# A decoder trunk with stick-breaking attention: scores by pairs of heads with q and k unstacked, and query blocks 0 and 1 as one unit

## The chip, the cores and the metric

The kernel runs on 1 core of one Trainium2 chip. The metric is device time in microseconds (us), from the start of one execution to its end. The kernel before was run three times.

## What is computed

The reference runs two layers over a residual stream of 512 positions by 1024. The first is multi-head latent attention with a causal softmax (called the MLA layer here). The second is stick-breaking attention with 16 heads of 64, which takes its keys and values from a product of the stream after the first layer. After each layer a gated embedding is added: `x + sigmoid(x @ W) * (p @ W')`. The change touches the second layer, whose core is this, for each block of 128 queries of each head:

```python
z = einsum('bhqd,bhkd->bhqk', qi, k) * scale
mask = s_idx[None, :] < t_idx[:, None]
log_beta = log_sigmoid(z)
log_one_minus = where(mask, log_sigmoid(-z), 0.0)
tail = cumsum(log_one_minus, reverse=True) - log_one_minus
a = where(mask, exp(log_beta + tail), 0.0)
o = einsum('bhqk,bhkd->bhqd', a, v)
```

Then `x + (o * silu(gate)) @ w_out`. All is float32.

## The kernel before, in words

Activations lie transposed: features on the 128 partitions, 512 positions along the free axis. A float32 product is made of three matmuls in the reduced format `float32r`, after each operand is split in two parts, high and low: high by high, high by low, low by high (`mm3`, L121 to L123). ScalarE (ACT) makes the high part by a cast, VectorE (DVE) or GpSimd (POOL) the low part by a subtraction (`split_w` for weights, L130 and L131; `split_act` for activations, L147 and L148).

The second layer goes in four groups of four heads. For each group `sb_group` makes values (`V`), keys and queries by products with weights that POOL first multiplies by a gain (L169 and L614). The products of the next group and the gate products (`gate2`) are handed out as filler, a chunk at a time, between the steps of the attention of the current group (`layer`, `windows`); after the last group the embedding product and the two big output products follow (`pp_gemm`, `out_ple`).

*Keys and queries before.* A head has 64 features, half of the 128 rows. The kernel stacks parts along the rows: for a key tile the upper half holds the high part and the lower half the low part (or the other way round), and each query has two tiles, one with the high part in both halves (tag `qk`) and one with the low part in both halves (tag `hat`). Two matmuls of 128 rows then give all products of the parts. Making this takes, for each chunk of two heads, two casts and two subtractions of 64 rows for the keys (L588 to L591) and four casts and four subtractions of 64 rows for the queries (L601 to L604).

*Attention before.* One step is one query block `j` (0 to 3) of one head (`sb_front`): two matmuls of (j+1)*128 columns, at least 256, into one of two PSUM buffers of tag `s` (L643, L644); two sigmoids on ACT (L648, L649); a scan from the right on DVE that multiplies the factors up (L650); a product on POOL (L652); and a masking of the diagonal block on POOL (`affine_select`, L653). The tiles have tag `e`, with six buffers, two for each step. Some steps later PE transposes the blocks (`pt_evac`, L522), ACT casts them out of PSUM (L527), DVE subtracts the low part (L528), and when a head's four blocks are there, `av` multiplies them with the values (L542).

The order of the instructions on each engine is set when the program is built: a scheduler with priorities (`high_priority`, `SB_PRIO`, `SB_FILL`) simulates the program and places every instruction. Each engine then runs its own list in order and waits at semaphores.

Of the kernel before, what the change touches and what calls it, by code (L numbers as in the profile page):

```python
# [43 lines left out]
SB_LEAD = (2, 3, 2)  # L44
# [12 lines left out]
SPREAD = "gst"  # L57
SPREAD_PLE = "gstt"

# [25 lines left out]
class Trunk:  # L85
    def __init__(self, ctx, tc, A):
        self.tc, self.nc, self.A = tc, tc.nc, A
        self.cp = ctx.enter_context(tc.tile_pool(name="cp", bufs=1))
        self.sp = ctx.enter_context(tc.tile_pool(name="sp", bufs=1))
        self.pp = ctx.enter_context(tc.tile_pool(name="pp", bufs=1, space=PSUM))  # L90
        self.dp = ctx.enter_context(tc.tile_pool(name="dp", bufs=1, space=DRAM))
        self.n = 0

    BUFS = {"A": 8, "B": 10, "qk": 8, "hat": 6, "gate": 8, "v": 2, "f": 6, "e": 6, "ws": 3, "wh": 2, "wl": 2, "R": 1,
            "sm": 16, "smg": 3, "g": 2, "s": 2, "t": 3, "o": 1}

    def t(self, shape, dt, tag):
        self.n += 1
        return self.sp.tile(shape, dt, tag=tag, name=f"{tag}{self.n}", bufs=self.BUFS[tag])

    def ps(self, shape, tag):
        self.n += 1
        return self.pp.tile(shape, F32, tag=tag, name=f"{tag}{self.n}", bufs=self.BUFS[tag])

    @contextmanager
# [88 lines left out]
    def setup(self):  # L194
# [6 lines left out]
        for _ in range(WARM):  # L201
# [10 lines left out]
                                compare_op=ALU.is_ge, fill=NEG, base=0, channel_multiplier=1)  # L212
        nc.gpsimd.affine_select(out=self.maskb[:, S - P:S], in_=self.maskb[:, S - P:S], pattern=[[-1, P]],
                                compare_op=ALU.is_ge, fill=1.0, base=-1, channel_multiplier=1)
        self.pt = []
        for i in range(2):
            pair = []
# [70 lines left out]
    def mla_in(self):  # L288
# [1 line left out]
        gc = self.const([P, NCOL], F32, "gc")  # L290
        self.gc = gc
        MC = (QL + KL) // P
        tags = "".join(x * self.BUFS[x] for x in "gst")
        acc = [self.ps([P, S], x) for x in tags[:MC]]
        xacts = []
        sqx = self.t([P, S], F32, "f")
# [216 lines left out]
    def pt_evac(self, h, j, e):  # L513
        nc = self.nc
        pt = self.pt[h % 2]
        if j == 0:
            self.e0 = e
            return
        blocks = [(self.e0, 0), (e, 0), (e, 1)] if j == 1 else [(e, c) for c in (1, 0, 2, 3)[:j + 1]]
# [3 lines left out]
        if j == 1:  # L523
            views = [x[:, 0:3 * P].rearrange("p (i q) -> p i q", q=P) for x in pt]
        else:
            views = [x[:, 3 * P:PTC].rearrange("p (i q) -> p i q", q=2 * P)[:, 0:j + 1, (j - 2) * P:(j - 1) * P] for x in pt]
# [51 lines left out]
    def sb_group(self, g, res):  # L578
        nc, A, v = self.nc, self.A, self.nc.vector
        ks, qs = {}, {}  # L580

        def k_evac(m, ps):
            kr = self.t([P, S], F32, "f")
            v.tensor_tensor(out=kr, in0=ps, in1=self.R2, op=ALU.mult)
            a = self.t([P, S], F32R, "B")
            b = self.t([P, S], F32R, "B")
            lo, hi = slice(0, HD), slice(HD, P)
            nc.scalar.copy(out=a[lo], in_=kr[lo])  # L588
            nc.scalar.copy(out=b[hi], in_=kr[hi])
            v.tensor_tensor(out=a[hi], in0=kr[lo], in1=f32(a[lo]), op=ALU.subtract)  # L590
            v.tensor_tensor(out=b[lo], in0=kr[hi], in1=f32(b[hi]), op=ALU.subtract)  # L591
            ks[2 * m], ks[2 * m + 1] = a, b

        def q_evac(m, ps):
            qr = self.t([P, S], F32, "f")
            v.tensor_tensor(out=qr, in0=ps, in1=self.R2, op=ALU.mult)
            for i, own in enumerate((slice(0, HD), slice(HD, P))):
                oth = slice(HD, P) if i == 0 else slice(0, HD)
                a = self.t([P, S], F32R, "qk")
                b = self.t([P, S], F32R, "hat")  # L600
                nc.scalar.copy(out=a[own], in_=qr[own])  # L601
                nc.scalar.copy(out=a[oth], in_=qr[own])
                v.tensor_tensor(out=b[own], in0=qr[own], in1=f32(a[own]), op=ALU.subtract)
                v.tensor_tensor(out=b[oth], in0=qr[own], in1=f32(a[own]), op=ALU.subtract)  # L604
                qs[2 * m + i] = (a, b)

        gkv = self.gc[:, C_KVLN:C_KVLN + NK]
        gsb = self.gc[:, C_SBLN:C_SBLN + NK]
# [15 lines left out]
            self.v_evac(V[:, t], ps, self.r2[:, t:t + 1])  # L624
            yield
        for m in (2 * g, 2 * g + 1):
            yield from self.gemm_gen(A["w_k"][m], m, self.x2, k_evac, gkv)
            yield
        for m in (2 * g, 2 * g + 1):
            yield from self.gemm_gen(A["w_sq"][m], m, self.x2, q_evac, gsb)  # L630
            yield
        res[:] = [qs, ks, V]

    def sb_prep(self, h, qs, ks, V):
        return qs[h] + (ks[h], V)

    def sb_front(self, h, j, qa, qb, k, V):
        nc, v = self.nc, self.nc.vector
        n = (j + 1) * P
        nn = max(n, 2 * P)  # L640
        js = slice(j * P, n)
        ps = self.ps([P, S], "s")
        nc.tensor.matmul(ps[:, 0:nn], lhsT=qa[:, js], rhs=k[:, 0:nn], start=True, stop=False)  # L643
        nc.tensor.matmul(ps[:, 0:nn], lhsT=qb[:, js], rhs=k[:, 0:nn], start=False, stop=True)  # L644
        om = self.t([P, S + 8], F32, "e")
        b = self.t([P, S + 8], F32, "e")
        nc.vector.memset(om[:, n:n + 1], 1.0)
        nc.scalar.activation(om[:, 0:n], ps[:, 0:n], AF.Sigmoid, scale=-(HD ** -0.5))  # L648
        nc.scalar.activation(b[:, 0:n], ps[:, 0:n], AF.Sigmoid, scale=HD ** -0.5)  # L649
        v.tensor_tensor_scan(out=om[:, 0:n][:, ::-1], data0=om[:, 0:n][:, ::-1], data1=self.maskb[:, S - n:S][:, ::-1],  # L650
                             initial=1.0, op0=ALU.mult, op1=ALU.max)
        nc.gpsimd.tensor_tensor(out=b[:, 0:n], in0=b[:, 0:n], in1=om[:, 1:n + 1], op=ALU.mult)  # L652
        nc.gpsimd.affine_select(out=b[:, js], in_=b[:, js], pattern=[[-1, P]], compare_op=ALU.is_ge, fill=0.0,  # L653
                                base=-1, channel_multiplier=1)
        return b

    def pp_gemm(self, i):
        nc, A = self.nc, self.A
# [56 lines left out]
    def layer(self, windows, prep, front, pair, prep_lead, lead, av_lag, off):  # L715
# [5 lines left out]
        for i in range(-prep_lead, NS + lead + av_lag):  # L721
            ip = i + prep_lead
            if ip < NS:
                g = ip // GS
                if ip % NT == 0:
                    with hp(offset=off[0]):
                        heads[ip // NT] = prep(ip // NT, *self.groups[g])
                n, gen = windows[g]
                while done[g] * GS < n * (ip % GS + 1):
                    next(gen, None)  # L730
                    done[g] += 1
                if ip % GS == GS - 1:
                    for _ in gen:
                        pass
            if 0 <= i < NS:
                with hp(offset=off[1]):
                    es[i] = front(i // NT, i % NT, *heads[i // NT])
            b = i - lead
            if 0 <= b < NS:
                with hp(offset=off[2]):  # L740
                    self.pt_evac(b // NT, b % NT, es.pop(b))
# [17 lines left out]
    def run(self):  # L759
# [183 lines left out]
```

## Time and profile before

| | us |
|---|---|
| three runs | 710.0, 712.96, 713.29 |
| median | 712.96 |
| span of the profiled execution | 709.4 |
| PE busy | 667.6 |
| DVE busy | 526.7 |
| ACT busy | 409.6 |
| POOL busy | 401.3 |

The span runs from the first to the last instruction of one execution that the hardware profiler took; no time outside the span is recorded for that execution. "Busy" is the time in which at least one instruction ran. A matmul's end is modelled, and consecutive matmuls overlap, so how fast PE gets along is read from the distance between the starts of neighbouring matmuls. PEld are weight loads, each ahead of its matmul. The first scores of the second layer start at 375 us, the last products with the values end at 610 us.

### The profile page before, as it was taken

To read this page: it belongs to the slowest core of one execution; us is meant where nothing else is said; L and a number is where in the kernel's file an instruction comes from. 1 tells how busy PE (TensorE), PEld (TensorE's weight loads), DVE (VectorE), ACT (ScalarE), POOL (GpSimd) and SP (SyncE) were. 2 spreads that over 40 slices of the span, in tenths; PEclk is the share of its full clock that TensorE was granted. 3 is DMA by queue.
4 is the path that set the end of the run, shared out by engine and by line. 5 is a ranking of instruction groups with operands and counts; after the bars stand their busy time and mean duration, and the time that the engine had idled before them with its cause. 6 is when DMAs were issued, how large, how long until landed. Compare 5 with 4: busy or idle time off the path is not lost.

```text
span 709.4 us, 10085 instructions
## 1 busy us (share of the span) xinstructions
PE 667.6 (94%) x3494; PEld 563.9 (79%) x3494; DVE 526.7 (74%) x966; ACT 409.6 (58%) x837; POOL 401.3 (57%) x371
## 2 busy tenths in 40 slices
PE   8899999899999999998898998999999988999997
PEld 6688878788868888887787876878887767888886
DVE  6758499999978866455579899799789788544432
ACT  7266586868878655453254667666466365622321
POOL 6638476775695430058545687787883998200131
PEclk9999999999999999999998999999999999999999
DMA  6232202010133113442231112111112121443231
GB/s 232 78 121 92 93 31 64 30 33 14 32 119 119 46 60 95 135 155 98 84 116 60 60 61 59 61 59 61 61 59 89 61 84 58 147 137 109 84 124 59
DMA packets 21474, 59.28 MB, mean 84 GB/s; under 512 B 2864, under 2 KB 3376, under 8 KB 21424
## 3 DMA queue, kind: packets, MB, share of 16 engines
q1 hardware_dynamic: 21424, 58.65, 25.8%
q8 instruction: 27, 0.44, 0.2%
q14 instruction: 23, 0.19, 0.1%
HBM read 54.45 MB, written 4.19 MB: 83 GB/s over the span
## 4 chain that ended last, share of the span: by engine, by line
PE 42%; DVE 25%; issue 14%; POOL 13%; ACT 4%; DMA 2%; SPq 0%; POOLq 0%; ACTq 0%; DVEq 0%
PE g L121 6%; PE g L123 6%; PE g L122 6%; POOL e L652 4%; PE t L121 3%; PE t L123 3%; PE t L122 3%; PE s L121 3%; PE s L123 3%; PE s L122 3%; POOL e L653 3%; DVE e L650 3%; DVE wl L131 2%; PE o L542 2%; DVE ptl L528 2%
## 5 line engine op out<-in xcount | busy, mean ns | idle before, releaser
L130 ACT CAST wh<-ws 128x1024 fp32r<-128x1024 f32 (+2 forms) x92 | 90.8, 987 | 105.9 <-issue 50.2
L131 DVE TENSOR_TENSOR wl<-ws,wh 128x1024 fp32r<-128x1024 f32 (+2 forms) x72 | 100.9, 1401 | 44.6 <-ACT wh L130 38.3
L121 PE MATMUL g<-A,wh 128*128 128x512 f32 x280 | 112.6, 402 | 4.0 <-ACT wh L322 4.0
L122 PE MATMUL g<-A,wh 128*128 128x512 f32 x280 | 112.4, 401 | 1.0 <-DVE A L148 0.9
L123 PE MATMUL g<-A,wl 128*128 128x512 f32 x280 | 110.7, 399 | 0.4 <-DVE wl L131 0.4
L652 POOL TENSOR_TENSOR e<-e,e 128x128 f32<-128x128 f32 (+1 forms) x64 | 62.4, 983 | 26.9 <-DVE e L650 12.7
L650 DVE TENSOR_TENSOR_SCAN e<-e,maskb 128x128 f32<-128x128 f32 (+1 forms) x64 | 71.1, 1125 | 8.5 <-ACT e L648 6.6
L522 PE MATMUL t<-ident,e 128*128 128x128 f32 x320 | 61.0, 278 | 11.7 <-POOL e L652 6.8
L709 POOL TENSOR_TENSOR f<-f,B 128x512 f32<-128x512 f32 x8 | 14.1, 1765 | 102.2 <-ACT f L707 102.0
L169 POOL TENSOR_TENSOR ws<-ws,gc 128x1024 f32<-128x1024 f32 x24 | 50.3, 2097 | 31.9 <-DMA ws<-in_w_k 10.0
L121 PEld LDWEIGHTS g<-A,wh 128*128 128x128 f32 x280 | 53.3, 190 | 15.0 <-ACT wh L322 5.1
L122 PEld LDWEIGHTS g<-A,wh 128*128 128x128 f32 x280 | 53.5, 191 | 12.1 <-DVE A L148 2.8
L123 PEld LDWEIGHTS g<-A,wl 128*128 128x128 f32 x280 | 53.1, 190 | 10.5 <-DVE wl L131 0.8
L522 PEld LDWEIGHTS t<-ident,e 128*128 128x128 f32 x320 | 39.8, 140 | 24.3 <-POOL e L652 9.6
L528 DVE TENSOR_TENSOR ptl<-t,pth 128x384 fp32r<-128x384 f32 (+1 forms) x96 | 55.1, 589 | 2.5 <-ACT pth L527 2.0
L527 ACT CAST pth<-t 128x384 fp32r<-128x384 f32 (+1 forms) x96 | 47.9, 522 | 7.9 <-PE t L522 7.5
L131 POOL TENSOR_TENSOR wl<-ws,wh 128x1024 fp32r<-128x1024 f32 (+2 forms) x20 | 41.0, 2052 | 18.9 <-ACT wh L130 18.9
L648 ACT ACTIVATE e<-s 128x128 f32<-128x128 f32 (+1 forms) x64 | 28.4, 444 | 35.4 <-POOL e L652 19.7
L568 ACT ACTIVATE e<-e,sm,smg 128x128 f32<-128x128 f32 (+1 forms) x64 | 42.1, 660 | 11.7 <-DVE sm L567 9.3
L653 POOL TENSOR_SCALAR_AFFINE_SELECT e<-e 128x128 f32<-128x128 f32 x64 | 44.8, 711 | 1.5
L572 POOL TENSOR_SCALAR e<-e,sm 128x384 f32<-128x384 f32 (+3 forms) x48 | 28.6, 603 | 26.7 <-DVE sm L570 18.2
L542 PE MATMUL o<-ptl,v 128*128 128x256 f32 (+2 forms) x128 | 40.7, 340 | 1.0 <-DVE ptl L528 1.0
(324 smaller groups left out, 1935.4 us busy)
## 6 DMA issues: line engine op xcount, KB each, us to landing
ws<-in_w_pg SPq DMA_DIRECT2D x16, 512.0 KB, 3.6
ws<-in_w_g SPq DMA_DIRECT2D x8, 512.0 KB, 3.2
ws<-in_w_o SPq DMA_DIRECT2D x16, 256.0 KB, 2.5
ws<-in_w_v SPq DMA_DIRECT2D x8, 512.0 KB, 3.6
ws<-in_w_k SPq DMA_DIRECT2D x8, 512.0 KB, 3.5
ws<-in_w_sq SPq DMA_DIRECT2D x8, 512.0 KB, 3.5
ws<-in_w_sg SPq DMA_DIRECT2D x8, 512.0 KB, 3.6
ws<-in_w_o SPq DMA_DIRECT2D x8, 512.0 KB, 3.6
```

Source lines behind the costliest of these rows:

```text
L121: mm(ps, lhsT=wh, rhs=xh, start=first, stop=False)
L122: mm(ps, lhsT=wh, rhs=xl, start=False, stop=False)
L123: mm(ps, lhsT=wl, rhs=xh, start=False, stop=last)
L130: nc.scalar.copy(out=wh, in_=src)
L131: lo_engine.tensor_tensor(out=wl, in0=src, in1=f32(wh), op=ALU.subtract)
L169: nc.gpsimd.tensor_tensor(out=ws, in0=ws, in1=gain.unsqueeze(2).to_broadcast((P, nk, P)), op=ALU.mult)
L522: nc.tensor.transpose(ps[:, i], src[:, c * P:(c + 1) * P], self.ident)
L528: nc.vector.tensor_tensor(out=views[1], in0=ps, in1=f32(views[0]), op=ALU.subtract)
L542: nc.tensor.matmul(ps[:, q0:S], lhsT=V[:, c, hh], rhs=rhs, start=(c == 0 and i == 0), stop=(c == NT - 1 and i == 1))
L650: v.tensor_tensor_scan(out=om[:, 0:n][:, ::-1], data0=om[:, 0:n][:, ::-1], data1=self.maskb[:, S - n:S][:, ::-1], initial=1.0, op0=ALU.mul ...
L652: nc.gpsimd.tensor_tensor(out=b[:, 0:n], in0=b[:, 0:n], in1=om[:, 1:n + 1], op=ALU.mult)
L653: nc.gpsimd.affine_select(out=b[:, js], in_=b[:, js], pattern=[[-1, P]], compare_op=ALU.is_ge, fill=0.0, base=-1, channel_multiplier=1)
```

## The change

1. Keys and queries are no longer stacked. For a chunk of two heads one tile holds the high parts of both (first head in rows 0 to 63, second in rows 64 to 127) and one the low parts: one cast and one subtraction of 128 rows each (`evac`, `split_act`).
2. Scores are made for two heads at a time (`sb_scores`). For each head there are three matmuls of 64 rows (high by high, high by low, low by high), placed by `tile_position` in rows 0 to 63 for the first head and 64 to 127 for the second, in turn. They write the two halves, one PSUM bank each, of a single tile `s2` that stays for the whole program; the tag `s` elsewhere takes these halves in turn.
3. Query blocks 0 and 1 become one unit of 512 columns (block 0 with key blocks 0 and 1, block 1 with key blocks 0 and 1), with a mask of its own, `maskp`, that makes key block 1 of query block 0 drop out and the scan start anew between the two. A pair of heads thus has three units of 512, 384 and 512 columns for each head, where a head had four steps of 128, 256, 384 and 512. The sigmoids take both heads in one instruction, scans and products stay one for each head, the masking is one for both heads (two for the first unit).
4. The loop is `sb_layer`, with a lead of one unit between scores and transposes; `pt_evac` is called by units in both layers. The `e` tiles hold two heads each, still six of them. The DMA scratch area is set to 1024 (`dynamic_dma_scratch_size`).

```diff
-    def sb_front(self, h, j, qa, qb, k, V):
-        nc.tensor.matmul(ps[:, 0:nn], lhsT=qa[:, js], rhs=k[:, 0:nn], start=True, stop=False)
-        nc.tensor.matmul(ps[:, 0:nn], lhsT=qb[:, js], rhs=k[:, 0:nn], start=False, stop=True)
...
+        def evac(to, tag):
+            def f(m, ps):
+                r = self.t([P, S], F32, "f")
+                v.tensor_tensor(out=r, in0=ps, in1=self.R2, op=ALU.mult)
+                to[m] = self.split_act(r, tag)
...
+    def sb_scores(self, u, qs, ks):
+        ps = self.s2
+        parts = [(0, 0, 2), (1, 2, 2)] if u == 0 else [(u + 1, 0, u + 2)]
+        terms = [(qs[0], ks[0]), (qs[0], ks[1]), (qs[1], ks[0])]
+        for j, c0, nb in parts:
+            for i, (q, k) in enumerate(terms):
+                for hh in range(2):
+                    rows = slice(hh * HD, (hh + 1) * HD)
+                    nc.tensor.matmul(ps[:, hh, c0 * P:(c0 + nb) * P], lhsT=q[rows, j * P:(j + 1) * P],
+                                     rhs=k[rows, 0:nb * P], start=i == 0, stop=i == 2, tile_position=(hh * HD, 0))
+    def sb_front(self, u, ps):
+        n = (4, 3, 4)[u] * P
+        om = self.t([P, 2, S + 8], F32, "e")
+        b = self.t([P, 2, S + 8], F32, "e")
+        v.memset(om[:, :, n:n + 1], 1.0)
+        nc.scalar.activation(om[:, :, 0:n], ps[:, :, 0:n], AF.Sigmoid, scale=-(HD ** -0.5))
+        nc.scalar.activation(b[:, :, 0:n], ps[:, :, 0:n], AF.Sigmoid, scale=HD ** -0.5)
+        for hh in range(2):
+            v.tensor_tensor_scan(out=x, data0=x, data1=mask[:, ::-1], initial=1.0, op0=ALU.mult, op1=ALU.max)
+            nc.gpsimd.tensor_tensor(out=b[:, hh, 0:n], in0=b[:, hh, 0:n], in1=om[:, hh, 1:n + 1], op=ALU.mult)
+        for d in ds:
+            nc.gpsimd.affine_select(out=d, in_=d, pattern=[[0, 2], [-1, P]], compare_op=ALU.is_ge, fill=0.0, base=-1,
+                                    channel_multiplier=1)
...
-        self.layer(windows, self.sb_prep, self.sb_front, pair2, *SB_LEAD, SB_PRIO)
+        self.sb_layer(windows, pair2, SB_LEAD, SB_PRIO)
```

The scheduler places the whole program anew, the first layer too. On PE, at the scores of query block 3 of a head in the second group, the order before has two matmuls of 128 rows (`s`) between products of the filler (`g`):

```order
L121 MATMUL g_5312<-wh_5218,A_3574 128x256
L122 MATMUL g_5312<-wl_5219,A_3574 128x256
L643 MATMUL s_5630<-B_4831,qk_5001 128x512
L644 MATMUL s_5630<-B_4831,hat_5002 128x512
L123 MATMUL g_5312<-wh_5218,A_3574 128x256
```

Now, at the same block of a pair of heads, six matmuls of 64 rows stand in one run between full-row matmuls of the filler (`g`) and of the product with the values (`o`):

```order
L140 MATMUL g_4674<-A_3636,wh_4670 128x512
L141 MATMUL g_4674<-A_3636,wl_4671 128x512
L653 MATMUL s_66<-B_4267,qk_4424 128x512 x2
L653 MATMUL s_66<-B_4268,qk_4424 128x512 x2
L653 MATMUL s_66<-B_4267,qk_4425 128x512 x2
L139 MATMUL g_4674<-A_3677,wh_4670 128x512
L569 MATMUL o_4824<-pth_112,v_3993 128x512
```

The 192 matmuls of 64 rows (L653) stand in 27 such runs. On DVE, before, at the queries of the last group, four subtractions of 64 rows (L603, L604) follow for each chunk of two heads on the product with the norm (L596); `wl` is a weight split, L650 a scan:

```order
L596 TENSOR_TENSOR f_5702<-g_5648,R_3761 128x512
L131 TENSOR_TENSOR wl_5835<-ws_5831,wh_5834 128x1024
L603 TENSOR_TENSOR hat_5705<-f_5702,qk_5704 64x512
L604 TENSOR_TENSOR hat_5705<-f_5702,qk_5704 64x512
L647 MEMSET e_6011 128x1
L647 MEMSET e_6049 128x1
L603 TENSOR_TENSOR hat_5711<-f_5702,qk_5710 64x512
L604 TENSOR_TENSOR hat_5711<-f_5702,qk_5710 64x512
L650 SCALAR_TENSOR_TENSOR e_5962<-e_5962,maskb 128x128
```

Now, at the same place, one subtraction of 128 rows (L166) stands there, after the product with the norm (L612), and the scans (L669) come in twos, one for each head:

```order
L612 TENSOR_TENSOR f_5449<-g_5424,R_3696 128x512
L669 SCALAR_TENSOR_TENSOR e_5589<-e_5589,maskp 128x512 x2
L576 TENSOR_TENSOR gate_5643<-o_5646,gate_5643 64x512
L149 TENSOR_TENSOR wl_5528<-ws_5524,wh_5527 128x1024
L166 TENSOR_TENSOR qk_5452<-f_5449,qk_5451 128x512
```

Three of four subtractions of the queries are gone from DVE's list there, and one of two of the keys (L590, L591) likewise.

## Rows read from the trace of the kernel before

**Rows 1.** The page, part 1: busy time, share of the span, instructions.
```profile
PE 667.6 (94%) x3494; PEld 563.9 (79%) x3494; DVE 526.7 (74%) x966; ACT 409.6 (58%) x837; POOL 401.3 (57%) x371
```
**Rows 2.** Windows: length, PE, PEld, DVE, ACT, POOL busy (instructions), PEclk, DMA, GB/s.
```profile
80.00:260.00 180.00, 170.96 (x988) 147.70 (x987) 158.75 (x448) 142.28 (x346) 115.86 (x113) 1.00 0.17 55
...
360.00:617.50 257.50, 239.63 (x1299) 202.56 (x1298) 222.31 (x316) 155.07 (x306) 184.69 (x169) 0.98 0.22 68
```
**Rows 3.** Waits of PE, 360 to 617.5 us: total, times, longest.
```profile
PE t L522 <- POOL e L652: 6.8, 8, 1.8
PE g L121 <- DVE v L496: 4.8, 2, 3.0
PE t L522 <- POOL e L653: 3.9, 10, 0.6
```
**Rows 4.** Windows inside the stage, columns as in rows 2.
```profile
360.00:405.00 45.00, 41.96 (x236) 37.45 (x235) 38.80 (x50) 23.84 (x47) 23.48 (x21) 0.92 0.23 71
...
560.00:600.00 40.00, 34.07 (x165) 26.94 (x163) 33.92 (x45) 21.66 (x45) 37.36 (x37) 0.96 0.21 67
```
**Rows 5.** Timeline of PE: start, length, line, shape; distances between starts count.
```profile
608.78 0.39 PE L542 MATMUL o<-ptl,v 128*128 128x512 f32 x1
609.01 0.33 PE L542 MATMUL o<-pth,v 128*128 128x384 f32 x1
609.18 0.34 PE L542 MATMUL o<-ptl,v 128*128 128x384 f32 x1
...
609.48 0.28 PE L542 MATMUL o<-ptl,v 128*128 128x256 f32 x1
609.60 0.28 PE L542 MATMUL o<-pth,v 128*128 128x256 f32 x1
```
**Rows 6.** Timeline of all engines around the only 64-row matmuls, in the first layer.
```profile
48.75 0.40 PE L123 MATMUL s<-wh,B 128*128 128x512 f32 x1
49.07 0.32 PEld L394 LDWEIGHTS t<-ident,f 64*128 64x128 f32 x4 [0.36 <-issue]
...
49.57 0.19 PEld L122 LDWEIGHTS t<-wl,B 128*128 128x128 f32 x1
```
**Rows 7.** Timeline of ACT: the copy that those 64-row matmuls read.
```profile
44.86 0.56 ACT L391 COPY f<-t 64x512 f32<-64x512 f32 x1
```
**Rows 8.** Lines of DVE by form, 360 to 617.5 us: busy, mean ns, idle before.
```profile
L650 DVE TENSOR_TENSOR_SCAN e<-e,maskb 128x512 f32<-128x512 f32 x16 | 25.8, 1611 | 3.0 <-ACT e L648 2.5 <-issue 0.5
...
L603 DVE TENSOR_TENSOR hat<-f,qk 64x512 fp32r<-64x512 f32 x16 | 15.0, 939 | 0.2
L650 DVE TENSOR_TENSOR_SCAN e<-e,maskb 128x256 f32<-128x256 f32 x16 | 15.0, 939 | 0.4 <-issue 0.3
L604 DVE TENSOR_TENSOR hat<-f,qk 64x512 fp32r<-64x512 f32 x16 | 13.7, 859 | 0.2
L650 DVE TENSOR_TENSOR_SCAN e<-e,maskb 128x128 f32<-128x128 f32 x16 | 11.5, 717 | 3.9 <-ACT e L648 2.8 <-ACT pth L527 1.0
...
L590 DVE TENSOR_TENSOR B<-f,B 64x512 fp32r<-64x512 f32 x8 | 7.1, 884 | 0.9 <-ACT B L588 0.7
...
L148 DVE TENSOR_TENSOR A<-gate,A 128x512 fp32r<-128x512 f32 x7 | 4.6, 688 | 0.3 <-ACT A L147 0.3
```
**Rows 9.** Lines of ACT by form, same stretch and columns.
```profile
L648 ACT ACTIVATE e<-s 128x512 f32<-128x512 f32 x16 | 9.7, 606 | 8.9 <-PE s L644 4.8 <-POOL e L652 3.7 <-PE t L522 0.5
...
L648 ACT ACTIVATE e<-s 128x128 f32<-128x128 f32 x16 | 4.6, 288 | 10.3 <-PE s L644 5.7 <-POOL e L652 4.5
```
**Rows 10.** Lines of POOL by form, same stretch and columns.
```profile
L653 POOL TENSOR_SCALAR_AFFINE_SELECT e<-e 128x128 f32<-128x128 f32 x64 | 44.8, 711 | 1.5
...
L652 POOL TENSOR_TENSOR e<-e,e 128x512 f32<-128x512 f32 x16 | 19.1, 1192 | 6.8 <-PE g L123 2.4 <-DVE e L650 1.6 <-ACT pth L527 1.5
```
**Rows 11.** Timeline of DVE ahead of the longest wait of PE.
```profile
381.61 2.29 DVE L604 TENSOR_TENSOR hat<-f,qk 64x512 fp32r<-64x512 f32 x1
...
384.87 0.46 DVE L496 SCALAR_TENSOR_TENSOR v<-g,r,v 128x256 fp32r<-128x256 f32 x1
```

More of the change, by code (lines that the diff above doesn't have):

```diff
@@ L92, in __init__ @@
         self.n = 0
+        self.turn = 0
+        self.s2 = self.pp.tile([P, 2, S], F32, tag="s2", name="s2", bufs=1)
     BUFS = {"A": 8, "B": 10, "qk": 8, "hat": 6, "gate": 8, "v": 2, "f": 6, "e": 6, "ws": 3, "wh": 2, "wl": 2, "R": 1,
-            "sm": 16, "smg": 3, "g": 2, "s": 2, "t": 3, "o": 1}
+            "sm": 16, "smg": 3, "g": 2, "t": 3, "o": 1}
     def t(self, shape, dt, tag):
@@ L99, in t, with half @@
         return self.sp.tile(shape, dt, tag=tag, name=f"{tag}{self.n}", bufs=self.BUFS[tag])
+    def half(self, shape):
+        self.turn = 1 - self.turn
+        n = 1
+        for x in shape[1:]:
+            n *= x
+        x = self.s2[0:shape[0], self.turn, 0:n]
+        if len(shape) == 3:
+            return x.rearrange("p (a b) -> p a b", b=shape[2])
+        if len(shape) == 4:
+            return x.rearrange("p (a b c) -> p a b c", b=shape[2], c=shape[3])
+        return x
     def ps(self, shape, tag):
         self.n += 1
+        if tag == "s":
+            return self.half(shape)
         return self.pp.tile(shape, F32, tag=tag, name=f"{tag}{self.n}", bufs=self.BUFS[tag])
@@ L214, in setup @@
                                 compare_op=ALU.is_ge, fill=1.0, base=-1, channel_multiplier=1)
+        self.maskp = self.const([P, S], BF16, "maskp")
+        nc.vector.memset(self.maskp, 0.0)
+        nc.vector.memset(self.maskp[:, P:2 * P], 1.0)
+        for c in (0, 3):
+            d = self.maskp[:, c * P:(c + 1) * P]
+            nc.gpsimd.affine_select(out=d, in_=d, pattern=[[-1, P]], compare_op=ALU.is_ge, fill=1.0, base=-1,
+                                    channel_multiplier=1)
         self.pt = []
@@ L292, in mla_in @@
         MC = (QL + KL) // P
-        tags = "".join(x * self.BUFS[x] for x in "gst")
+        tags = "ggssttt"
         acc = [self.ps([P, S], x) for x in tags[:MC]]
@@ L511, in head_t, with pt_evac @@
         return hi, lo
-    def pt_evac(self, h, j, e):
+    def pt_evac(self, h, u, e, e0=None):
         nc = self.nc
         pt = self.pt[h % 2]
[L516 to L519, printed above, removed]
+        if u == 0:
+            blocks = [(e, c) for c in (0, 2, 3)] if e0 is None else [(e0, 0), (e, 0), (e, 1)]
+        else:
+            blocks = [(e, c) for c in (1, 0, 2, 3)[:u + 2]]
         ps = self.ps([P, len(blocks), P], "t")
@@ L580, in sb_group @@
         ks, qs = {}, {}
[L582 to L605, printed above, removed]
+        def evac(to, tag):
[3 more added lines that the diff above has]
+                to[m] = self.split_act(r, tag)
+            return f
         gkv = self.gc[:, C_KVLN:C_KVLN + NK]
@@ new lines, in sb_front @@
+    def sb_front(self, u, ps):
+        nc, v = self.nc, self.nc.vector
+        n = (4, 3, 4)[u] * P
[4 more added lines that the diff above has]
+        nc.scalar.activation(b[:, :, 0:n], ps[:, :, 0:n], AF.Sigmoid, scale=HD ** -0.5)
+        mask = self.maskp if u == 0 else self.maskb[:, S - n:S]
+        for hh in range(2):
+            x = om[:, hh, 0:n][:, ::-1]
+            v.tensor_tensor_scan(out=x, data0=x, data1=mask[:, ::-1], initial=1.0, op0=ALU.mult, op1=ALU.max)
+            nc.gpsimd.tensor_tensor(out=b[:, hh, 0:n], in0=b[:, hh, 0:n], in1=om[:, hh, 1:n + 1], op=ALU.mult)
+        if u == 0:
+            ds = [b[:, hh, 0:S].rearrange("p (i c) -> p i c", c=P)[:, 0::3] for hh in range(2)]
+        else:
+            ds = [b[:, :, n - P:n]]
+        for d in ds:
+            nc.gpsimd.affine_select(out=d, in_=d, pattern=[[0, 2], [-1, P]], compare_op=ALU.is_ge, fill=0.0, base=-1,
+                                    channel_multiplier=1)
+        return b
@@ new lines, in sb_layer @@
+    def sb_layer(self, windows, pair, lead, off):
+        hp = self.tc.high_priority
+        NU = 3
+        GS = NU * GH // 2
+        bs = {}
+        for i in range(NU * NH // 2 + lead):
+            if i < NU * NH // 2:
+                m, u = divmod(i, NU)
+                g = i // GS
+                qs, ks, V = self.groups[g]
+                with hp(offset=off[1]):
+                    bs[i] = self.sb_front(u, self.sb_scores(u, qs[m], ks[m]))
+                n, gen = windows[g]
+                for _ in range(n * (i % GS + 1) // GS - n * (i % GS) // GS):
+                    next(gen, None)
+                if i % GS == GS - 1:
+                    for _ in gen:
+                        pass
+            b = i - lead
+            if b >= 0:
+                m, u = divmod(b, NU)
+                e = bs.pop(b)
+                with hp(offset=off[2]):
+                    for hh in range(2):
+                        self.pt_evac(2 * m + hh, u, e[:, hh])
+                if u == NU - 1:
+                    with hp(offset=off[3]):
+                        for hh in range(2):
+                            self.av(2 * m + hh, self.groups[m // 2][2])
+                    pair(m)
@@ L739, in layer @@
             if 0 <= b < NS:
-                with hp(offset=off[2]):
-                    self.pt_evac(b // NT, b % NT, es.pop(b))
+                h, j = divmod(b, NT)
+                if j > 0:
+                    with hp(offset=off[2]):
+                        self.pt_evac(h, j - 1, es.pop(b), es.pop(b - 1) if j == 1 else None)
             c = b - av_lag
```

30 lines of the change are left out of this document (8 added, 22 removed).

## The prediction

> **What bounds the kernel now.** I read the page first: PE is busy 94% of the span, no other engine above 74% [rows 1]. So time can come out in two ways only: fewer or cheaper matmuls, or less waiting of PE. Then the windows by stage: the change works in the second layer's attention, 360 to 617.5 us, where PE is busy for 239.6 of 257.5 us and so idle for 17.9; DVE is busy for 222.3 of it, 86%, POOL for 184.7 [rows 2]. Next the waits of PE in this stage. Three sorts make 15.5 of the 17.9 us: 10.7 us where a transpose (L522) waits for POOL's product or masking of the `e` tile, and 4.8 us where a product waits for a PSUM buffer that DVE is late to empty [rows 3]. Then the same stage in pieces: the granted clock is 0.92 on average in the first 45 us and 0.96 in the 40 us from 560 us on, where POOL is at 93% [rows 4]. The clock's shortfall is worth 0.08 x 45 = 3.6 and 0.04 x 40 = 1.6 us. Idle time and clock together, 23 us, are all that less waiting can give back here.
>
> The stage after it is not touched. The first layer computes the same, though its order is drawn up anew: PE is idle there for 9.0 of 180 us [rows 2], so I take 0, with 4 us either way.
>
> **The sum is made against the span of the profiled execution, 709.4 us.** No time outside it is recorded; the median of the runs is 3.6 us above it, and I add the change to the median, 712.96.
>
> **Part 1, the scores on PE.** Neighbouring matmuls start 0.23 us apart for 512 columns, 0.17 for 384, 0.12 for 256 [rows 5]. Before, a head has two matmuls each of 256, 256, 384 and 512 columns: 2 x (0.12 + 0.12 + 0.17 + 0.23) = 1.28 us, 20.5 us for 16 heads. After, a pair of heads has 12 matmuls of 256 columns, 6 of 384 and 6 of 512, all of 64 rows, in turn in the upper and lower half. No row of before has two halves at work at once, so I bound it. If they don't overlap, a pair costs 12 x 0.12 + 6 x 0.17 + 6 x 0.23 = 3.84 us, 30.7 us for 8 pairs: +10.2 us. If two halves run wholly side by side, half of that, 15.4 us: -5.1 us. Less would need a weight load to take longer than its matmul: the four 64-row loads in the trace take 0.32 us together with 0.14 for one, so they follow each other every 0.06 us [rows 6], two in the 0.12 us of the shortest matmul. That is the nearest row, and by it the loads don't stand in the way: I take -5.1 us.
>
> The Trainium skill, in "TensorE: Matmul & The Clock Gate", part 3 on packing small matmuls, says that matmuls in different row groups run at once, and gives a measured speed-up of 3.07 for four tiles. No run here shows it; by that share of the ideal, an estimate, two halves would give 1.54, so 20 us for the scores and a total near 709 us.
>
> **Part 2, going in and out of the 64-row matmuls.** The kernel before has one such passage, four small transposes in the first layer. The last full matmul ahead of them starts at 48.75 and takes its 0.23; the next weight load that runs beside a full-row matmul, so that matmul's start, is at 49.57. Of the 0.82 us, 0.23 are the full matmul and 4 x 0.06 the small ones; 0.35 us are lost [rows 6]. The first small load sits idle for 0.36 us with "issue" as the cause, and what it reads was ready long before: the copy on ACT ended at 44.86 + 0.56 = 45.42 [rows 7]. So this isn't a wait for data but the price of changing the row arrangement and changing back. After, there are 27 runs of 64-row matmuls: 27 x 0.35 = +9.5 us. The least is 0, where PE would have waited anyway; I take 9.5, since PE is at 93% there.
>
> The Trainium skill says so too ("TensorEngine Tiling (Array Packing)", Key Properties): changing the tiling mode drains TensorE. It speaks against this change, and the trace agrees, with 0.35 us for both ways.
>
> So PE's own work grows by 4.4 us, and the change has to earn its gain from the waits.
>
> **Part 3, the other engines.** DVE loses the stacked subtractions: 15.0 + 13.7 for the queries, 2 x 7.1 for the keys, 42.9 us; it gets 16 subtractions of 128 rows at 0.69, 11.0 us. Scans: 16 of 128 and 16 of 256 columns go, 11.5 + 15.0, and 16 of 512 come, 25.8: -0.7 us [rows 8]. Net -33 us of DVE's 222. ACT loses as many casts, which wait beside these, and its sigmoids get cheaper: 288 ns for 128 columns and 606 for 512 are 0.83 ns a column and some 0.18 us for each instruction, and 48 instructions do what 128 did [rows 9]. POOL has 16 products of 512 columns in place of 16 of 128 and 16 of 256, about even, and 32 maskings of 256 columns for 64 of 128. One of 128 took 711 ns; for 256 the bounds are 0.71 and 1.42, and I take 0.9, since a product on POOL needs 1.19 us for 512 and so little for each added column [rows 10]: 29 us for 44.8, -16 us.
>
> What does PE get of it? The wait of 4.8 us for the values' PSUM buffer: in its longest case DVE is in the middle of stacked subtractions, one of them 2.29 us long, and the values come after, at 384.87 [rows 11]. With two subtractions for eight there this wait goes, and the low clock that follows it (3.6 us) with it: the granted clock is either 2.4 or 1.2 GHz, so a mean of 0.92 over 45 us is 7 us at half clock, behind that idle stretch. That is 8.4 us. The 10.7 us behind POOL: its queue gets shorter by a tenth and the six `e` tiles now hold three units of two heads, where they held three steps of one; but a unit's own chain is longer (two sigmoids of 1024 columns at about 1.03 us each by this slope, a scan of 1.6, a second for the other head, two products of 1.2 and a masking of 0.9: some 6.5 us to the second head's diagonal block, where a step of 512 needed 0.6 + 0.6 + 1.6 + 1.2 + 0.7 = 4.7). With only one unit of lead, the next unit's scores and the filler have to cover that; and as `s2` holds a single unit, the next scores wait for both sigmoids, behind what else ACT has queued. I take half, 5 us. Together -13 us; the bounds are -23, all of it, and +3 if the longer chain isn't covered.
>
> **Sum:** -5.1 + 9.5 - 13 + 0 = -8.6 us. Span 700.8, median 704.4 us. This goes with 698 to 709.
>
> **Rivals.**
> 1. *The passages cost little and the waits go* (0.17). If the scheduler's runs lie where PE would have stood anyway, 3 us are left of the 9.5, and if the engines are as much relieved as their sums say, 18 of the 23 us return: -5.1 + 3 - 18 = -20, 693 us. For it: DVE falls from 86% to some 74%. Against: a chain, not a load, is what the transposes wait for.
> 2. *The halves overlap only in part* (0.16). Halfway between the bounds the scores cost +2.6: 2.6 + 9.5 - 13 = -0.9, 712 us. For it: nothing in the trace shows two halves at once. Against: the loads fit. The share of the Trainium skill's packing section would lie between this and the forecast.
> 3. *The halves follow each other* (0.12), slower: each of the 192 matmuls takes its full slot, at L653. +10.2 + 9.5 - 13 = +6.7, 719.7 us. It decides as soon as the scores cost over 24 us in all (15.4 + 8.6), that is, where the second of two halves starts later than about half a slot after the first.
> 4. *The waits stay* (0.15): the longer chain of a unit takes the place of the queue; transposes wait for the second head's masking and nothing is won from waits: -5.1 + 9.5 = +4.4, 717.4 us. For it: one unit of lead, one tile of scores.
>
> **The numbers.** The forecast has 0.40. What a measurement of this kernel can tell from no change is 0.5%, 3.6 us, so faster means under 709.4. Faster: nearly all of the forecast, all of rival 1, some of 2: 0.59. Slower (over 716.5): rivals 3 and most of 4, and a little of the rest: 0.24. The same: 0.17. The range reaches from rival 1 to just short of rival 3: 693 to 719.
>
> **What would show it.** The two matmuls of a pair at L653 start under 0.08 us apart, with the next pair a full slot later (part 1; 0.12 or more apart everywhere is rival 3). The weight load behind each run of L653 and the first one in it stand alone, some 0.35 us for both (part 2). In the stage, DVE is busy about 190 us and PE idle about 8, the products' wait behind the values' subtraction gone (part 3). It is wrong if transposes at L549 wait for POOL by over 10 us, or if the first layer's stage moves by over 4.

## The result, and the profile after

The changed kernel takes 743.4 us (median of 4 runs, 741.4 to 746.4) beside 711.5 for the kernel before (4 runs): a ratio of 1.0456 (95% interval 1.041 to 1.050). It is slower by 32 us, where 8.6 us less was forecast, and outside the range.

The page of the kernel after, part 1 (answers to [rows 1]):

```profile
span 744.7 us, 9929 instructions
...
PE 686.2 (92%) x3558; PEld 567.8 (76%) x3558; DVE 499.9 (67%) x880; ACT 391.2 (53%) x727; POOL 390.2 (52%) x325
```

DVE, ACT and POOL have less to do, as the change says; PE is busy for 18.6 us longer and idle for 16.7 us longer. The question is in which stage. Three landmarks divide the program: the last value product of the first layer, the first score of the second layer, its last value product. Before, they start at 262.3, 375.4 and 609.6 us; windows between them (to 0.4 us behind a last start) give the stages. First the kernel before (length, then PE, PEld, DVE, ACT, POOL busy with instructions, PEclk, DMA share, GB/s):

```profile
80.00:262.70 182.70, 173.66 (x1002) 150.07 (x1001) 161.09 (x450) 143.43 (x348) 117.91 (x113) 1.00 0.17 54
...
262.70:375.40 112.70, 107.20 (x515) 90.24 (x515) 68.34 (x75) 49.25 (x75) 42.58 (x24) 0.98 0.37 114
375.40:610.00 234.60, 216.73 (x1198) 183.59 (x1197) 202.30 (x295) 141.97 (x286) 177.04 (x165) 0.98 0.20 63
610.00:709.40 99.40, 95.30 (x444) 79.68 (x442) 42.30 (x51) 31.38 (x45) 14.39 (x8) 1.00 0.36 117
```

and the same four stages after:

```profile
80.00:299.40 219.40, 196.58 (x1050) 166.81 (x1048) 159.96 (x451) 151.74 (x355) 116.81 (x114) 0.95 0.15 51
...
299.40:416.60 117.20, 106.06 (x499) 87.31 (x498) 65.86 (x73) 44.27 (x66) 42.49 (x25) 0.96 0.33 106
416.60:647.10 230.50, 216.80 (x1247) 177.44 (x1247) 181.65 (x212) 121.96 (x181) 167.91 (x117) 0.99 0.20 62
647.10:744.70 97.60, 93.51 (x436) 78.19 (x434) 40.17 (x49) 29.24 (x41) 14.60 (x8) 1.00 0.37 119
```

The attention that was rewritten is 4.1 us shorter (234.6 to 230.5). The first layer, which computes exactly what it did, is 36.7 us longer. Its engines do the same work; PE is idle for 22.8 us instead of 9.0, and its clock is 0.95 instead of 1.00, worth 0.05 x 219 = 11 us; the other 12 us are 48 more matmuls recorded in the stretch (0.23 us each for 512 columns), filler that the longer layer took in. The stage behind it repays little of that: it has 16 matmuls fewer, but PE is idle for 11.1 us there instead of 5.5. What PE waits for there, before and after, 80 to 300 us (total, times, longest):

```profile
PE s L121 <- DVE sm L564: 3.2, 4, 1.3
```

```profile
PE s L139 <- DVE sm L591: 16.8, 15, 4.8
```

The score matmuls of the first layer wait for DVE's masked row maximum, the reader of the scores. The timeline of the kernel before shows how it was. Two first score matmuls (tag `s`) start before either result is read, then come both reductions on DVE:

```profile
80.67 0.37 PE L121 MATMUL s<-qk,qk 96*128 96x256 f32 x1
...
81.24 0.36 PE L121 MATMUL s<-qk,qk 96*128 96x256 f32 x1
...
82.34 0.28 DVE L564 CUSTOM_DVE_ANT_0 e<-s,mask 128x128 f32<-128x128 f32 x1
...
82.55 0.42 DVE L564 CUSTOM_DVE_ANT_0 e<-s,mask 128x256 f32<-128x256 f32 x1
```

After, the two alternate strictly, all 64 times in this layer; a stretch of it:

```profile
130.00 0.43 DVE L591 CUSTOM_DVE_ANT_0 e<-s,mask 128x256 f32<-128x256 f32 x1 [0.46 <-PE s L141]
...
130.49 0.69 PE L139 MATMUL s<-qk,qk 96*128 96x384 f32 x1 [0.53 <-DVE sm L591]
...
130.98 0.52 PE L140 MATMUL s<-qk,qk 96*128 96x384 f32 x1
...
131.30 0.52 PE L141 MATMUL s<-qk,qk 96*128 96x384 f32 x1
...
131.86 0.56 DVE L591 CUSTOM_DVE_ANT_0 e<-s,mask 128x384 f32<-128x384 f32 x1 [0.23 <-PE s L141]
...
132.48 0.80 PE L139 MATMUL s<-qk,qk 96*128 96x512 f32 x1 [0.66 <-DVE sm L591]
```

Scores at 130.49 start when the reduction of the scores before them is through, the next reduction starts when these are done, and so on. The second cost can be read here as well: L140 and L141 start 0.32 us apart, where 384 columns took 0.17 [rows 5]. That is the lower of PE's two clocks, 1.2 instead of 2.4 GHz: the granted clock from 130.4 to 132.5 us is 0.50, behind a wait of 2.9 us for the same reduction that ended at 129.34.

The cause is the sentence of the change that the prediction passed over: the tag `s` "elsewhere takes these halves in turn". Two buffers became two halves of one tile, and a user of one half now waits for the users of the other, although each half is a PSUM bank of its own.

### The profile page after: what moved, and what is told of

It is laid out like the page before. It is cut to its first block, busy times and chain, and to the rows that moved or that the text cites. A ratio compares the mean times of both kernels' runs of the same rounds, so it can differ in the third digit from the quotient of the medians.

```text
span 744.7 us, 9929 instructions
## 1 busy us (share of the span) xinstructions
PE 686.2 (92%) x3558; PEld 567.8 (76%) x3558; DVE 499.9 (67%) x880; ACT 391.2 (53%) x727; POOL 390.2 (52%) x325
## 4 chain that ended last, share of the span: by engine, by line
PE 57%; DVE 16%; POOL 11%; issue 7%; ACT 7%; DMA 2%; SPq 0%; ACTq 0%; POOLq 0%; DVEq 0%
PE g L139 8%; PE g L141 8%; PE g L140 8%; PE t L139 4%; PE o L569 4%; PE t L141 4%; PE t L140 4%; POOL e L670 4%; PE s L139 3%; PE t L549 3%; PE s L141 3%; PE s L140 3%; DVE e L669 2%; DVE wl L149 2%; DVE e L591 2%
## 5 line engine op out<-in xcount | busy, mean ns | idle before, releaser
L148 ACT CAST wh<-ws 128x1024 fp32r<-128x1024 f32 (+2 forms) x92 | 90.3, 983 | 129.7 <-issue 42.5
L149 DVE TENSOR_TENSOR wl<-ws,wh 128x1024 fp32r<-128x1024 f32 (+2 forms) x72 | 102.6, 1426 | 37.1 <-ACT wh L148 35.7
L141 PE MATMUL g<-A,wl 128*128 128x512 f32 x280 | 111.1, 401 | 2.4 <-DVE wl L149 1.4
L140 PE MATMUL g<-A,wh 128*128 128x512 f32 x280 | 111.6, 399 | 0.0
L670 POOL TENSOR_TENSOR e<-e,e 128x512 f32<-128x512 f32 (+1 forms) x48 | 68.8, 1452 | 13.6 <-DVE e L669 8.4
L549 PE MATMUL t<-ident,e 128*128 128x128 f32 x320 | 62.9, 287 | 12.4 <-POOL e L676 6.8
L141 PEld LDWEIGHTS g<-A,wl 128*128 128x128 f32 x280 | 53.4, 191 | 14.9 <-DVE wl L149 3.1
L140 PEld LDWEIGHTS g<-A,wh 128*128 128x128 f32 x280 | 53.2, 190 | 10.2 <-issue 0.6
L549 PEld LDWEIGHTS t<-ident,e 128*128 128x128 f32 x320 | 41.3, 146 | 24.0 <-POOL e L676 9.3
L669 DVE TENSOR_TENSOR_SCAN e<-e,maskb 128x384 f32<-128x384 f32 (+1 forms) x32 | 47.9, 1537 | 7.4 <-ACT e L664 7.4
L569 PE MATMUL o<-pth,v 128*128 128x256 f32 (+2 forms) x128 | 42.5, 342 | 0.4 <-ACT pth L554 0.4
L139 PE MATMUL s<-qk,qk 96*128 96x256 f32 (+1 forms) x64 | 25.9, 405 | 17.1 <-DVE sm L591 16.8
```

The source lines that it names most:

```text
L139: mm(ps, lhsT=wh, rhs=xh, start=first, stop=False)
L140: mm(ps, lhsT=wh, rhs=xl, start=False, stop=False)
L141: mm(ps, lhsT=wl, rhs=xh, start=False, stop=last)
L148: nc.scalar.copy(out=wh, in_=src)
L149: lo_engine.tensor_tensor(out=wl, in0=src, in1=f32(wh), op=ALU.subtract)
L569: nc.tensor.matmul(ps[:, q0:S], lhsT=V[:, c, hh], rhs=rhs, start=(c == 0 and i == 0), stop=(c == NT - 1 and i == 1))
```

## The experiments

The theory is that this sharing is the whole loss and that the rest of the change gains a little. The rival: the loss comes from the new attention code (its order, its passages, its longer unit) and the first layer is only displaced.

**The kernel before, with nothing but the shared tile** (outside the second layer's steps `s` is half of a pair tile):

```diff
+        if tag == "s" and self.s2 is not None:
+            return self.half(shape)      # s2[:, turn], turn = 1 - turn
```

> The kernel before, with one edit: outside the loop of the stick-breaking steps the tag s is the two halves of one tile, as in the changed kernel. Theory A (one tile makes its users wait for each other: the first layer's scores lose their second buffer): first layer's last product with the values at about 299 us where it was 262, the whole at 742 to 750 us. Rival B (the loss comes from the units of the transposes or from the new order, not from the tile): within 5 us of before, 707 to 716.

Measured: 745.8 us, ratio 1.049 (1.044 to 1.054). The row of waits, 80 to 300 us:

```profile
PE s L147 <- DVE sm L590: 17.2, 15, 4.8
```

The same wait, as often, and the whole loss, without any of the new attention; the first layer's last value product starts at 299.8 us, as the theory had it. The attention is that of before, and yet its stage is 5.3 us shorter than before, with 24 matmuls fewer (filler that now runs earlier):

```profile
414.40:643.70 229.30, 212.84 (x1174) 178.54 (x1175) 200.42 (x293) 140.57 (x285) 174.04 (x165) 0.99 0.20 63
```

So the 4.1 us by which the rewritten attention is shorter in the changed kernel do not show a gain of the rewriting; only the whole time of a kernel without the sharing does.

**The changed kernel with two tiles of one bank each** instead of two halves; the sigmoids then go head by head:

```diff
-        self.s2 = self.pp.tile([P, 2, S], F32, tag="s2", name="s2", bufs=1)
+        self.s2 = [self.pp.tile([P, S], F32, tag=f"s2{i}", name=f"s2{i}", bufs=1) for i in range(2)]
```

> The changed kernel with two tiles of one bank each in place of one of two banks; scores of the two heads go to one each, and the sigmoids are one for each head (96 instructions for 48, some 9 us more of ACT at 0.18 us each). Theory A: the waits of the first layer's scores for DVE (16.8 us) go, the first layer ends some 37 us earlier, the whole is at 703 to 712 us. Rival B: 738 to 746 us.

Measured: 716.3 us, 1.008 (1.005 to 1.011). The first layer's last value product is back at 262.6 us, which the first theory wanted; the whole is 4 us over its range. With a tile for each head the scheduler now lists the two heads' scores apart, in 48 runs instead of 27, mostly of one half alone:

```profile
572.91 0.78 PE L653 MATMUL s<-B,qk 64*128 64x384 f32 x3
573.62 0.49 PE L140 MATMUL g<-A,wh 128*128 128x512 f32 x1
574.05 0.78 PE L653 MATMUL s<-B,qk 64*128 64x384 f32 x3
```

Three matmuls of one half take 0.71 us from their start to the next full matmul. This becomes a measurement beside the next run, where six take 0.72.

**The changed kernel with the pair tile only while the second layer's steps run**, and two ordinary `s` buffers in all other stages:

```diff
-        self.s2 = self.pp.tile([P, 2, S], F32, tag="s2", name="s2", bufs=1)
+        self.spool()          # pool with two buffers of tag s
...
+        self.spool(True)      # pool with the pair tile
         self.sb_layer(windows, pair2, SB_LEAD, SB_PRIO)
+        self.spool()
```

> The changed kernel, with the single two-bank tile only during the loop of the stick-breaking steps; everywhere else the tag s has its two buffers again. All other parts of the change stay. Theory A: 698 to 712 us; the sum of the prediction's three parts would put it at 703. Rival B: 738 to 746 us. Rival C (the single tile costs in the steps' loop too, as the next scores wait for both sigmoids): 715 to 725 us, with waits of the scores L664 for ACT.

Measured: 707.2 us, 0.9952 (0.992 to 0.998). The four stages:

```profile
80.00:264.00 184.00, 176.38 (x1015) 152.27 (x1014) 159.54 (x450) 143.25 (x348) 119.26 (x115) 1.00 0.18 56
264.00:379.10 115.10, 109.74 (x537) 92.78 (x535) 67.87 (x73) 47.39 (x71) 44.06 (x25) 0.99 0.37 115
379.10:607.90 228.80, 215.47 (x1248) 175.97 (x1247) 185.79 (x212) 121.91 (x181) 167.14 (x117) 0.99 0.20 63
607.90:705.50 97.60, 93.52 (x436) 78.20 (x434) 40.18 (x49) 29.26 (x41) 14.59 (x8) 1.00 0.36 119
```

The first layer has its old length to 1.3 us. What is left of the change is worth 0.5%, 3.4 us. The third theory of this run, that the single tile costs in the steps' loop too, falls: PE has no wait at the scores (L664) in that stage. This kernel (called the mended one below) shows what the prediction's other terms were worth.

**The mended kernel with each head's three score matmuls listed in a row**, instead of the heads in turn:

```diff
-            for i, (q, k) in enumerate(terms):
-                for hh in range(2):
+            for hh in range(2):
+                for i, (q, k) in enumerate(terms):
```

> As e3_pool, with the six score matmuls of a block in another order: three of the first head, then three of the second, in place of in turn. If two halves run at once only where neighbours use different rows: 4 of 6 matmuls stand alone, the scores cost some 10 us more (15.4 to about 26 us), total 8 to 12 us over e3_pool. If the engine's queue finds the other half by itself or PE would wait anyway: within 3 us of e3_pool.

Measured: 708.96 us, 0.9969 (0.994 to 0.999). From the full matmul ahead of the 12 matmuls of 256 columns (377.04) to the one of 378.50 behind them it is the same 1.46 us as in the mended kernel (378.94 to 380.40): listed three by three they still go in pairs. That the list is as written shows where a run ends after two matmuls, at 424.69: it is 0.43 us to the next full matmul, as long as a run of four listed in turn takes in the mended kernel (426.57), so both are of one half.

**The mended kernel with q and k stacked again**, two matmuls of 128 rows for each head, pairs and units kept:

```diff
-                    nc.tensor.matmul(ps[:, hh, ...], lhsT=q[rows, ...], rhs=k[rows, 0:nb * P],
-                                     start=i == 0, stop=i == 2, tile_position=(hh * HD, 0))
+                    nc.tensor.matmul(ps[:, hh, ...], lhsT=q[i][:, ...], rhs=k[:, 0:nb * P], start=i == 0, stop=i == 1)
```

> The version with the pair tile only inside the second layer's loop, with q and k stacked again and two 128-row score matmuls for each head, as before the change; pairs and units stay. Theory A (the 64-row scores cost PE 5.4 us, of which the passages are the larger part, and PE's own time sets this stage): without them the ratio to before falls from 0.995 to about 0.988 (702 us), PE's busy time between 360 and 617 falls by about 5. Theory B (what the unstacking takes from VectorE and ScalarE is what shortened PE's waits): the copies and subtractions return, VectorE is at 215 or more in that stretch, PE's waits rise from 13 to 18 and the ratio stays at 0.993 to 1.0.

Measured: 720.6 us, 1.0163 (1.012 to 1.021), worse than either theory. The stage and PE's waits in it, 360 to 617.5 us:

```profile
360.00:617.50 257.50, 229.77 (x1259) 195.85 (x1258) 226.20 (x253) 145.55 (x218) 176.27 (x120) 0.98 0.20 62
```

```profile
PE t L560 <- POOL e L704: 15.3, 10, 3.2
PE g L150 <- DVE v L533: 4.1, 1, 4.1
PE o L580 <- DVE e L691: 2.5, 1, 2.5
PE t L560 <- POOL e L698: 2.1, 3, 1.0
```

So the scores in halves cost PE's time and yet are worth some 15 us, through what DVE (226.2 us busy, 206.4 in the mended kernel) and ACT (145.6, 134.2) no longer have to do; the two were not separated. Pairs and units alone, without them, lose 12 (0.0163 x 710).

**The same with a lead of two units:** `SB_LEAD = 2`.

> The stacked version in pairs of heads (1.0163 of before), with the transposes two steps behind the scores instead of one. Theory A (its PE waits come from the distance: a step of two heads gives the chain sigmoid, scan, product, masking too little room when VectorE is also busy with the stacking): the waits of 17.4 us behind GpSimd fall by 10 or more and the ratio falls to about 1.000. Theory B (VectorE has too much to do: 226 us of 257, and no distance changes that): the ratio stays between 1.010 and 1.020.

Measured: 717.6 us, 1.0085 (1.005 to 1.012), between the two theories and nearer to the second. The waits of the transposes stay at 16.7 us (17.4), so the distance isn't what they hang on; where the rest of the small gain comes from was not pursued.

**The mended kernel with a lead of two units:** `SB_LEAD = 2`.

> The version with the pair tile only inside the second layer's loop, with the transposes two steps behind the scores instead of one. Theory A (one step is too short for sigmoid, scan, product and masking, which is why the transposes wait for GpSimd): the waits of 9.5 us fall below 3 and the ratio falls from 0.995 to about 0.983. Theory B (GpSimd's throughput or the order of its queue, not the distance, makes them wait): the ratio stays within 0.99 to 1.0, and the end of the layer has one more step to drain, so that it may even rise.

Measured: 710.96 us, 1.0024 (0.999 to 1.006). The transposes wait for POOL as in the mended kernel, 9.8 us. More distance gives nothing; the time is rather longer.

**The mended kernel without POOL's maskings** (the diagonal blocks then stay unmasked):

```diff
-        for d in ds:
-            nc.gpsimd.affine_select(out=d, in_=d, pattern=[[0, 2], [-1, P]], compare_op=ALU.is_ge, fill=0.0, base=-1,
-                                    channel_multiplier=1)
```

> The version with the pair tile only inside the second layer's loop, and GpSimd's 32 maskings of the diagonal blocks (0.87 us each) left out: this part of the computation is not done. Theory A (the transposes wait for GpSimd because its queue is full): the two groups of transposes that wait for GpSimd, 9.5 us together, fall below 3, and the ratio falls from 0.995 to about 0.983. Theory B (the step is late as a whole, scan and sigmoids with it, and the wait is only put down to its last link): the waits pass to other groups and the ratio is 0.990 to 0.996.

Measured: 705.5 us, 0.9935 (0.990 to 0.997). POOL has 30 us less to do from 360 to 617.5 us, and the transposes wait nearly as long, now for the product:

```profile
PE t L560 <- POOL e L681: 8.9, 9, 2.8
PE g L150 <- DVE v L533: 1.7, 1, 1.7
```

**The same, with the diagonal masked by matmuls on PE:**

```diff
+                nc.tensor.matmul(ps[:, hh, (c0 + nb - 1) * P:(c0 + nb) * P], lhsT=self.idb, rhs=self.dmask, ...)
```

> As the run without the maskings, but with the diagonal masked on PE: 64 matmuls of 128 columns that add -30000 to the masked scores behind each burst. At 0.06 us each they cost PE 3.8 us. Theory A (GpSimd's queue): -9.5 + 3 + 3.8, a ratio of about 0.991. Theory B (the step is late as a whole): 0.998 to 1.002.

This kernel does not compute the right attention, so it only prices the instructions. Measured: 711.0 us, 1.0023 (0.999 to 1.005). Against the run without masks, 0.0088 x 710 = 6.2 us for 64 matmuls (with some 3 us of uncertainty either way), about 0.10 each where 0.06 was expected: more than POOL's maskings cost.

**The mended kernel with the transposes listed later on PE**, between products that need nothing from POOL:

```diff
-SB_PRIO = (0, 100, 0, 100)
+SB_PRIO = (0, 100, -200, 100)
```

> The version with the pair tile only inside the second layer's loop (0.9952 of before), with the transposes listed later on PE, between products that need nothing from GpSimd (their priority lowered by 200). Theory A (they stand in PE's list a few matmuls too early, and products behind them could run meanwhile): the 9.5 us of waits behind GpSimd fall below 4 and the ratio falls to about 0.988. Theory B (the products run out as well, or what waits for the transposes is late in its turn): the ratio stays at 0.993 to 1.000.

Measured: 704.1 us, 0.9890 (0.986 to 0.992), the fastest version here. The waits, 360 to 617.5 us:

```profile
PE t L560 <- POOL e L687: 3.5, 4, 1.9
PE t L560 <- POOL e L681: 3.5, 2, 3.2
```

They fall to 7.0 us, not below 4, while the time is what the first theory gave.

**The kernel before, with the same edit:**

> The kernel before, with only the transposes of the second layer listed later on PE (their priority lowered by 200). Theory A (what this move gives, 0.6% on the changed second layer, has to do with the list and not with the change): the ratio to before is 0.990 to 0.995, and the 10.7 us of waits behind GpSimd shrink. Theory B (before, with one head in a step and three steps between scores and transposes, the list holds enough between them): 0.998 to 1.003.

Measured: 713.2 us, 1.0015 (0.999 to 1.004): nothing. The transposes' waits for POOL do shrink, from 10.7 to 6.7 us, but 4.8 us of waits for DVE stand in their place. The move helps only with the new attention.

**The mended kernel with -300** instead of -200:

> The version with the pair tile only inside the second layer's loop, with the transposes' priority lowered by 300 instead of 200, below the products. Theory A (the later the better while products are left): 0.982 to 0.988. Theory B (GpSimd's queue is reordered as well and what waits for the transposes becomes late): 0.99 or more.

Measured: 710.3 us, 0.9977 (0.995 to 1.000). The transposes no longer wait for POOL but come too late themselves:

```profile
PE o L580 <- DVE ptl L566: 5.0, 1, 5.0
PE t L560 <- DVE ptl L566: 3.0, 4, 1.9
```

## Why the prediction was wrong

**The step that failed** is in the second paragraph, the term 0 of the sum: "The first layer computes the same, though its order is drawn up anew ... so I take 0, with 4 us either way." It measured +36.7 us to the layer's last value product. The text of the change named the cause, that the tag `s` takes the halves of one tile in turn; what then becomes of the first layer, where one buffer was read while the other was written, was not asked. Inside the steps' loop the prediction did see it ("as `s2` holds a single unit, the next scores wait for both sigmoids"), where PE turned out not to wait for it. The prediction's own test, "if the first layer's stage moves by over 4", is what failed. The run with only the shared tile gives the loss to the full; with two tiles in place of two halves, and in the mended kernel, the first layer has its old length. The cause is shown from both sides. None of the rivals had it: all four were about the rewritten attention.

The other terms are read from the mended kernel.

**Part 1, right.** The halves run wholly side by side, apart from the passages. The timeline of PE in the mended kernel around a run of 12 matmuls of 256 columns, and around one of 6 of 384:

```profile
378.94 0.28 PE L152 MATMUL g<-wh,A 128*128 128x256 f32 x1
379.15 0.98 PE L664 MATMUL s<-B,qk 64*128 64x256 f32 x12
380.06 0.50 PE L150 MATMUL g<-wh,A 128*128 128x256 f32 x2
380.40 0.28 PE L151 MATMUL g<-wl,A 128*128 128x256 f32 x1
...
402.50 0.79 PE L664 MATMUL s<-B,qk 64*128 64x384 f32 x6
403.22 0.50 PE L150 MATMUL g<-A,wh 128*128 128x512 f32 x1
```

From 378.94 to 380.40 there are 1.46 us. Three full matmuls of 256 columns fall into them, 0.36; 1.10 are left for 12 half matmuls, which one by one would need 12 x 0.12 = 1.44. The six of 384 take 0.72 us until the next full one, and three alone took 0.71 (the run with two tiles): the second half costs nothing. Rivals 2 and 3 fall. The share that the prediction worked out from the Trainium skill ("TensorE: Matmul & The Clock Gate", part 3), 1.54 for two halves, is not what was measured here, which is 2 without the passages.

**Part 2, right.** Of the 1.10 us, 6 pairs take 6 x 0.12 = 0.72; 0.38 are the passage in and out, for which 0.35 was taken. It is 27 runs, as said. Read in the same way, from the full matmul ahead to the second one behind, a run of six costs 0.92 us with 384 columns and 1.10 with 512. Together the scores cost 8 x 1.10 + 8 x 0.92 + 8 x 1.10 us and three more passages where a unit is split in two (1.1): 26.1 us, against 20.5 before. PE's own work grows by 5.6 us (4.4 forecast).

**Part 3, too large.** Expected were 13 us from the waits and the clock. The stage of the mended kernel and PE's waits in it, beside [rows 2], [rows 3] and [rows 4]:

```profile
360.00:617.50 257.50, 244.17 (x1386) 200.13 (x1384) 206.40 (x230) 134.16 (x199) 177.06 (x121) 0.99 0.23 72
...
360.00:405.00 45.00, 42.49 (x264) 35.85 (x262) 36.35 (x39) 21.83 (x32) 27.24 (x19) 1.00 0.23 71
```

```profile
PE t L560 <- POOL e L687: 6.5, 6, 1.9
PE t L560 <- POOL e L681: 3.0, 5, 1.3
PE g L150 <- DVE v L533: 1.8, 1, 1.8
```

The wait for the values' buffer falls from 4.8 to 1.8 us and the clock of the first 45 us rises from 0.92 to 1.00 (3.6 us): of the 8.4 us some 6.6 came. The waits behind POOL fall from 10.7 to 9.5, not by 5: there the fourth rival was right. All idle time falls by 4.6 us, from 17.9 to 13.3; with the clock 8.2 us instead of 13. Against +5.6 on PE that leaves -2.6 in this sum; measured are -3.4 (the ratio). The difference of 0.8 us is inside the interval, 2.1 us either way. Of the signs named for this part, DVE at about 190 us and PE idle for about 8 did not come (206.4 and 13.3); the wait behind POOL stayed under 10 us.

Sizes behind it were off. DVE falls by 16 us, not 33: a subtraction of 128 rows takes 1.05 us, not the 0.69 taken from L148 (6 us for the 16), and work that was counted as unchanged grows, the weight splits from 50.4 to 54.4 us and a scan of 384 columns from 1235 to 1477 ns. POOL falls by 7.6, not 16: a product of 512 columns takes 1.57 us, not 1.19, so that these products cost 49.5 us where those of 128, 256 and 512 columns before cost 44.5; the forecast had them about even. The lines of the mended kernel, 360 to 617.5 us (busy, mean ns of one, idle before):

```profile
L177 DVE TENSOR_TENSOR qk<-f,qk 128x512 fp32r<-128x512 f32 x8 | 8.4, 1052 | 0.0
```

```profile
L681 POOL TENSOR_TENSOR e<-e,e 128x512 f32<-128x512 f32 x32 | 49.5, 1565 | 9.1 <-DVE e L680 5.7 <-ACT pth L565 3.4
```

The masking (872 ns for 0.9) and the sigmoid of 1024 columns (1.02 us for 1.03) were right. And what relief there was came from the unstacking: without it, in the stacked run, DVE is busy for 226 us of the same stretch, more than the 222 before, and the waits behind POOL grow to 17.4.

Why the waits behind POOL stayed, although its queue is shorter, the runs answer in part: it is neither POOL's load (30 us less moved 0.6 of them) nor the distance (a lead of 2 moved none). In part it is where the transposes stand in PE's list: the move by 200 takes 2.5 of the 9.5 us of waits and 0.6% of the time, and by 300 is too far. What the other 7.0 us hang on, and why the time fell by more than these waits, is open.

## What to carry to other kernels

Before a stage is counted at nothing because it computes the same, follow every buffer that the change renames into it: two buffers that become two halves of one tile can turn a ping-pong into a strict alternation, and every user of the old tag pays, far from the code that was rewritten. A shared tile belongs into a scope of its own, as in the mended kernel. And where a change relieves an engine that PE waits for, read the waits as a chain: what is taken from its last link alone, POOL's maskings here, hardly comes back.

## What was not expected of the hardware

Matmuls of the two row halves need not be listed in turn: with three of one head and then three of the other, a run is as short (1.46 us between the same neighbours, both ways).

An operation's time is not fixed by its shape. The subtraction into `A` of 128 rows took 688 ns before [rows 8] and 937 in the mended kernel. Without POOL's maskings, 16 scans of 512 columns on DVE took 1419 ns instead of 1696, here first with and then without them:

```profile
L680 DVE TENSOR_TENSOR_SCAN e<-e,maskb 128x512 f32<-128x512 f32 x16 | 26.5, 1696 | 7.2 <-ACT e L675 7.2
...
L566 DVE TENSOR_TENSOR ptl<-t,pth 128x384 fp32r<-128x384 f32 x32 | 16.5, 541 | 2.9 <-ACT pth L565 2.9
```

```profile
L680 DVE TENSOR_TENSOR_SCAN e<-e,maskb 128x512 f32<-128x512 f32 x16 | 22.0, 1419 | 8.1 <-ACT e L675 8.0
...
L566 DVE TENSOR_TENSOR ptl<-t,pth 128x384 fp32r<-128x384 f32 x32 | 16.5, 542 | 0.1
```

The subtraction L566, one of whose inputs lies in PSUM, doesn't move. The Trainium skill ("GPSIMD Engine Reference", Specifications) says that GpSimd shares its SBUF interface with VectorE and that they contend when a DVE instruction has two SBUF inputs. These two lines agree. Other instructions of DVE with two SBUF inputs do not: the 16 scans of 512 columns with the mask `maskp` took 1511 ns with the maskings and 1526 without, the subtractions of L177 1052 and 1159. So the runs do not show that this contention is the cause.
